# A two-layer SSD and pooling step on one core: another order of the load queue, weight preparation spread over scans 0 to 5, and one step more between a prepared half's loads and their sum

## The chip, the cores and the metric

The kernel runs on one core of a Trainium2 chip. The metric is the device time of one execution in microseconds (us). The kernel before took 1622.03 us, the median of three runs (1621.26 to 1628.29). The engines are called as in the profile: PE (matrix multiplies; PEld its weight loads), DVE and ACT (vector and scalar work on tiles), POOL, and SP, which here only issues DMAs.

## The reference

One inference step of two mixer layers with a prompt of 1024 tokens and 8 sample sequences of 8 tokens. Layer 0 is a Mamba-2 layer (SSD), layer 1 a causal pooling layer; each is adaLN, RMSNorm, projection, mixer, gate, out projection, residual. Cut to what matters here:

```python
mod = silu(c) @ ada_w[i] + ada_b[i]              # shift, scale, gate of layer i
hn  = rmsnorm(x, norm_g[i]) * (1 + scale) + shift
# layer 0
z, xbc, dt = split(hn @ w_in)                    # z 2048, x|B|C 4096, dt 32
xs, B, C = split(silu(causal_conv4(xbc)))        # 8 groups of 4 heads, state 128
acum = cumsum(dt * A)                            # in chunks of 128 tokens
y = (C B^T * exp(acum_t - acum_s)) (xs dt) + C exp(acum) h_prev     # scan over chunks
x = x + gate * (groupnorm((y + d*xs) * silu(z)) * norm_g) @ w_out
# layer 1: pooled windows 2, 4, 8, 16 of u, a product per group, * silu(z), @ pool_w_out
```

It also returns the new states (ssm, conv and pool, for prompt and sample).

## The kernel before, in words

All of it is fp32 work done on PE by splitting an operand into a high and a low float32r part; a product is three matmuls (hi x hi, lo x hi, hi x lo). The helper on L103 records every matmul, L106 every transpose, so in the profile PE's rows have these lines and are told apart by their tiles: st (fast pairs of the projections), mm (in-projections of a group during the scans), tr, S and y (the scan), am (adaLN), op (out products), pl (pool). The two out projections are computed by seven block products instead of eight, so for some of them blocks of the weight have to be added or subtracted first.

The program runs in stages. A front part of 108 us sets up the norms; the fast pairs last to about 349 us; eight scans, one for each group of heads, last from there to about 860 us; the out product of layer 0 overlaps the last scans and lasts to about 1000 us; the pool layer and its out product take the rest. Each scan g has four steps p of 256 tokens (L1630 on). While scan g runs, PE is kept at work with units of the next group's in-projection (`units`, L1607, numbers of units in the table PACE; in scans 6 and 7 the units are of the out product) and with blocks of adaLN (`ada`).

- **Weight stream.** A list of weight blocks is loaded in order: `stream_raw` (L130) issues a 512 KB load on SP into one of three buffers wr, L137 for projection weights (wr<-win), L141 for adaLN weights (wr<-adaG). `stream_split` makes of it wh (ACT, L160) and wl (DVE, L161). `stream_next` splits the next block and loads those behind it. `ada_block` (L260) takes two raw blocks for sixteen am matmuls, ACT copies the result to mp (L273), two small matmuls follow, and DVE makes shf and scl of it (L292, L293).
- **Weight preparation.** `prep_step` (L1176) is called at each scan step with (g, p), and once ahead of the scans with None. It works on halves of summed weight blocks, 16 in all (NPREP is 8 weights). For one half: two loads of 256 KB (SP, L1195, wp<-wout), the sum of the two (DVE, L1186), the high part (ACT, L1181), the low part (DVE, L1182), and a store of 512 KB to DRAM (SP, L1183, wpd<-wp). The out product reads them back with `ow_load` (L1205). The table PREP (L42) says how many halves are begun at a step; the sum of a half belongs to the call after the one that loads it, the split and store to the call after that.
- **Decay broadcast.** `scan_ac` (L539) loads the running sums of a step, broadcast to all partitions (SP, L542, acb<-acd, 512 KB), into the one buffer acb. ACT reads it for ea (L575), M (L580) and, last, cd (L583). The next acb load can go only then.
- **Convolution and its stores.** `proj_evict` moves mm out of PSUM (ACT, L456, L458); the conv is ACT L364 and DVE L366 to L369; POOL gathers the new conv state into ncv (L371) and SP stores it (L407). `silu_burst` (L412) does the silu of the next group's tiles between two scans, and the transposes tr of the next scan read them. Some tiles were made earlier and are reloaded (L430, xbc<-xbd, the table MOVED).
- **Scan.** POOL L602 and DVE L603 carry the state h; L606 stores the last one (hpT). L1132 loads gated rows (b<-gyd) for the out product, ACT L1140 splits them.

What sets the order: PE's instructions in the scans are pinned in program order. On ACT, DVE, POOL and SP a scheduler places the instructions by program order and by its own estimate of when their operands are ready. Each engine then works through its list in order and waits at each row for what the row needs. SP's list is in order as well, and a DMA there may also wait for one of a ring of eight completion semaphores, that is for the landing of the eighth DMA before it.

Of the kernel before, what the change touches and what calls it, by code (L numbers as in the profile page):

```python
# [40 lines left out]
NPREP = 8  # L41
PREP = {None: 4, (0, 0): 2, (0, 1): 2, (0, 2): 1, (0, 3): 1, (1, 3): 1, (2, 3): 2, (3, 3): 2, (4, 3): 1}  # L42
OWTAGS = (("wr", "wr"), ("wh", "wl"), ("wh", "wl"))
# [68 lines left out]
class Build:  # L112
# [147 lines left out]
    def ada_block(self, src, raws=None):  # L260

        nc = self.nc
# [7 lines left out]
        if own:  # L270
            self.slots.free(*own)
        mp = self.cp.tile([P, 256], F32, tag="mp", bufs=1, name=self.name("mp"))
        nc.scalar.activation(mp, pm[:, :256], AF.Copy)  # L273
# [103 lines left out]
    def proj_open(self, g):  # L377
# [3 lines left out]
        return dict(g=g, scv=scv, ncv=ncv, ti=(16 + g, 24 + g, 2 * g, 2 * g + 1), out=[])  # L381

    def proj_begin(self, G, ii):
        nc = self.nc
        raw = self.raw_tile()
        nc.gpsimd.memset(raw[:, 0:3], 0.0)
        nc.gpsimd.tensor_copy(raw[:, 1027:1115].rearrange("p (b w) -> p b w", w=11)[:, :, 0:3], G["scv"][:, ii])
        return raw

    def proj_end(self, G, ii, raw, ahead=False):  # L390
        dst = self.slots.get("xbc")
        self.conv_tile(G["ti"][ii], raw, dst, G["ncv"][:, ii])
        g, nt = G["g"], self.io["ncT"][G["g"]]
# [8 lines left out]
        if ii == 3 and not ahead:  # L402
            kept = [i for i in range(4) if (g, i) not in MOVED]
            for a in kept:
                if a - 1 not in kept:
                    n = next(i for i in range(a, 5) if i not in kept)
                    self.nc.sync.dma_start(nt[:, a:n], G["ncv"][:, a:n])  # L407

# [15 lines left out]
    def proj_group(self, G):  # L424

        nc = self.nc
        for ii in range(4):
            if (G["g"], ii) in MOVED:
                dst = self.slots.get("xbc")
                nc.sync.dma_start(dst, self.xbd[G["g"], ii])  # L430
                G["out"].append(dst)
                continue
            w = self.stream_next()
            raw = self.proj_begin(G, ii)
# [153 lines left out]
    def scan_state(self, s, p):  # L588

        nc, gp = self.nc, self.gs  # L590
# [4 lines left out]
        for cc in range(2):  # L595
            h, Sv = s.h[-1], S[:, 256 * cc:256 * cc + 256].rearrange("p (r q) -> p r q", r=4)
            hn = gp.tile([P, 4, 64], F32, tag="h", bufs=3, name=self.name("h"))
# [6 lines left out]
            s.h.append(hn)  # L604
        if p == 3:
            nc.sync.dma_start(self.io["hpT"][s.g], hn.rearrange("p r q -> p (r q)"))  # L606

# [568 lines left out]
    def prep_step(self, key):  # L1176

        nc = self.nc
        summed, loaded = self.preps
        for i, h, op, t, v in summed:  # L1180
# [6 lines left out]
        new = []  # L1187
        for _ in range(min(PREP.get(key, 0), 2 * NPREP - self.prepn)):
# [7 lines left out]
            new.append((i, h, op, t, v))  # L1196
        self.preps = loaded, new

# [134 lines left out]
    def run(self):  # L1333
# [22 lines left out]
        with tc.tile_pool(name="cp", bufs=1) as self.cp, tc.tile_pool(name="wp", bufs=1) as self.wp, \  # L1356
# [11 lines left out]
            self.wpd = [dr.tile([P, 2, 8, P], F32, tag=f"wpd{i}", name=f"wpd{i}") for i in range(NPREP)]  # L1368
            self.preps, self.prepn = ([], []), 0
            self.x1d = [dr.tile([P, TOK], F32, tag=f"x1d{i}", name=f"x1d{i}") for i in range(8)]  # L1370
# [186 lines left out]
    def fills(self):  # L1557
# [9 lines left out]
        for j, _ in enumerate(pr):  # L1567
# [4 lines left out]
            if j < 8:  # L1572
                yield
        self.ow_load()
        self.x = [None] * 8
        yield from self.out_fill()
# [40 lines left out]
    def scan(self, s, fill):  # L1617

        g = s.g
        last, after = self.scans[g - 1] if g else None, self.scans[g + 1] if g < 7 else None  # L1620
        for p in range(4):
# [10 lines left out]
            if p < 3:  # L1632
                self.scan_decay(s, p + 1)
                if p < 2:
                    self.scan_ac(s, p + 2)
                elif after:
                    self.scan_ac(after, 0)
            self.units(fill, b)
            if p == 3 and after:
                self.silu_burst(after)  # L1640
            self.scan_y(s, p, self.sample_y if p == 3 else None)
            if p == 2:
                self.sample_front(s)
                self.sample_inter(s)
# [7 lines left out]
            elif p == 3:  # L1652
                if g < 7:
                    self.sample_decay(s)
                else:
                    self.gate_rows(s)
            self.units(fill, min(c, 1))
            for _ in ada:
                pass
# [345 lines left out]
```

## Time and profile before

| | before |
|---|---|
| median of three runs | 1622.03 us (1621.26 to 1628.29) |
| profiled execution | 1621.86 us |
| its span (what the trace shows) | 1620.0 us |
| PE busy | 1568.6 us, 97% |
| DVE, ACT, POOL busy | 1307.7 (81%), 803.4 (50%), 491.8 (30%) us |
| DMA moved | 295.80 MB, mean 183 GB/s |

The span is the time in the trace from the first to the last instruction; the 1.86 us between it and the execution's own time lie around it. A wait is written as "engine, line, what it waited for: total us, times, longest". A row of a timeline is the start in us, the length, the engine, the line, the operation, what it writes and reads, the shape, the count, and in brackets the idle time before it with its releaser. For a row that groups several instructions the length is that of the group. PEclk in a table of windows is the TensorE clock that was granted, 1.00 at full speed.

### The profile page before, as it was taken

To read this page: it belongs to the slowest core of one execution; us is meant where nothing else is said; L and a number is where in the kernel's file an instruction comes from. 1 tells how busy PE (TensorE), PEld (TensorE's weight loads), DVE (VectorE), ACT (ScalarE), POOL (GpSimd) and SP (SyncE) were. 2 spreads that over 40 slices of the span, in tenths; PEclk is the share of its full clock that TensorE was granted. 3 is DMA by queue.
4 is the path that set the end of the run, shared out by engine and by line. 5 is a ranking of instruction groups with operands and counts; after the bars stand their busy time and mean duration, and the time that the engine had idled before them with its cause. 6 is when DMAs were issued, how large, how long until landed. Compare 5 with 4: busy or idle time off the path is not lost.

```text
span 1620.0 us, 31607 instructions
## 1 busy us (share of the span) xinstructions
PE 1568.6 (97%) x12495; PEld 1508.3 (93%) x12495; DVE 1307.7 (81%) x2095; ACT 803.4 (50%) x1426; POOL 491.8 (30%) x508
## 2 busy tenths in 40 slices
PE   8999999997999999999998999999999999999997
PEld 6899999996988888988887999999999999999997
DVE  6876787857888889888896999888889867667876
ACT  6663343446667667666653367523232334233355
POOL 0134555511121221111110003765666640000231
PEclk9999999998999999999998999999999999999999
DMA  8422222378675675677889763233323379466673
GB/s 350 164 100 94 87 84 85 111 245 289 225 251 186 207 255 187 215 262 246 320 282 306 194 161 118 71 115 113 115 102 105 108 236 380 135 179 178 162 164 115
DMA packets 118651, 295.80 MB, mean 183 GB/s; under 512 B 22860, under 2 KB 46824, under 8 KB 118504
## 3 DMA queue, kind: packets, MB, share of 16 engines
q1 hardware_dynamic: 110440, 270.32, 48.8%
q0 software_dynamic: 5760, 19.01, 6.7%
q10 hardware_dynamic: 2304, 4.46, 0.7%
q8 instruction: 98, 1.61, 0.4%
q14 instruction: 49, 0.40, 0.1%
HBM read 222.93 MB, written 68.59 MB: 180 GB/s over the span
## 4 chain that ended last, share of the span: by engine, by line
PE 77%; DVE 7%; DMA 7%; ACT 5%; issue 2%; POOL 1%; SPq 0%; DVEq 0%; ACTq 0%; POOLq 0%
PE st L103 32%; PE mm L103 18%; PE op L103 15%; PE y L103 3%; DMA wp<-wout 2%; PE pl L103 2%; DMA acb<-acd 2%; PE S L103 2%; PE am L103 1%; ACT M L580 1%; DMA wr<-pout 1%; PE tr L103 1%; PE ms L103 1%; DVE raw L366 1%; PE tr L106 1%
## 5 line engine op out<-in xcount | busy, mean ns | idle before, releaser
L103 PE MATMUL op<-b,w 128*128 128x272 f32 x2688 | 350.0, 292 | 15.6 <-ACT w L1231 7.1
L103 PEld LDWEIGHTS op<-b,w 128*128 128x128 f32 x2688 | 343.4, 191 | 21.3 <-ACT w L1231 7.7
L103 PE MATMUL st<-hh,w 128*128 128x272 f32 x1664 | 323.2, 289 | 0.0
L103 PEld LDWEIGHTS st<-hh,w 128*128 128x128 f32 x1664 | 265.4, 189 | 0.3 <-issue 0.3
L103 PE MATMUL st<-t,w 128*128 128x272 f32 x1872 | 242.7, 288 | 1.3 <-POOL w L197 1.3
L103 PE MATMUL st<-hl,w 128*128 128x272 f32 x832 | 240.6, 289 | 0.0
L103 PEld LDWEIGHTS st<-t,w 128*128 128x128 f32 x1872 | 237.4, 188 | 1.5 <-POOL w L197 1.5
L103 PE MATMUL mm<-hh,wh 128*128 128x364 f32 (+1 forms) x528 | 183.7, 348 | 2.1 <-ACT wh L160 2.1
L103 PE MATMUL mm<-hh,wl 128*128 128x364 f32 (+1 forms) x528 | 175.1, 332 | 0.3 <-DVE wl L161 0.3
L103 PE MATMUL mm<-hl,wh 128*128 128x364 f32 (+1 forms) x528 | 174.9, 331 | 0.0
L103 PEld LDWEIGHTS st<-hl,w 128*128 128x128 f32 x832 | 156.8, 188 | 0.0
L195 ACT ACTIVATE w<-wr 128x512 fp32r<-128x512 f32 x104 | 65.6, 631 | 179.6 <-PE st L103 143.7
L602 POOL TENSOR_TENSOR hd<-h,cd 128x256 f32<-128x256 f32 x56 | 58.5, 1044 | 225.8 <-DVE h L603 142.5
L103 PEld LDWEIGHTS mm<-hh,wh 128*128 128x128 f32 x528 | 100.7, 191 | 14.0 <-issue 9.5
L366 DVE SCALAR_TENSOR_TENSOR raw<-raw,vec,raw 128x1112 f32<-128x1112 f32 x64 | 91.2, 1426 | 17.5 <-ACT raw L364 17.0
L197 POOL TENSOR_TENSOR w<-wr,w 128x512 fp32r<-128x512 f32 x52 | 91.4, 1757 | 44.2 <-ACT w L195 44.2
L103 PEld LDWEIGHTS mm<-hl,wh 128*128 128x128 f32 x528 | 100.7, 191 | 0.7
L103 PEld LDWEIGHTS mm<-hh,wl 128*128 128x128 f32 x528 | 100.4, 190 | 0.8 <-DVE wl L161 0.8
L1256 DVE SCALAR_TENSOR_TENSOR x<-op,gat,x 128x272 f32<-128x272 f32 (+1 forms) x160 | 73.1, 480 | 26.9 <-PE op L103 23.0
L580 ACT ACTIVATE M<-acb,tka 128x128 f32<-128x128 f32 x256 | 81.1, 389 | 24.6 <-PE y L103 13.1
L974 DVE TENSOR_TENSOR u<-st,u 128x272 f32<-128x272 f32 x174 | 67.6, 411 | 31.6 <-PE st L103 29.8
L197 DVE TENSOR_TENSOR w<-sw,w 128x512 fp32r<-128x512 f32 x78 | 79.2, 1016 | 14.6 <-ACT w L195 14.4
(279 smaller groups left out, 3210.5 us busy)
## 6 DMA issues: line engine op xcount, KB each, us to landing
wr<-win SPq DMA_DIRECT2D x48, 512.0 KB, 4.1
acb<-acd SPq DMA_DIRECT2D x32, 512.0 KB, 4.6
wr<-pin SPq DMA_DIRECT2D x32, 512.0 KB, 3.5
wr<-pout SPq DMA_DIRECT2D x28, 512.0 KB, 4.5
wr<-wout SPq DMA_DIRECT2D x20, 512.0 KB, 5.7
wr<-pout POOLq DMA_DIRECT2D x20, 512.0 KB, 5.9
x<-xT SPq DMA_DIRECT2D x16, 544.0 KB, 6.7
zsd<-z SPq DMA_DIRECT2D x16, 544.0 KB, 2.7
```

The lines of the kernel that those rows point to most:

```text
L103: return self.pin(self.build.nc.tensor.matmul(*a, **k))
L106: return self.pin(self.build.nc.tensor.transpose(*a, **k))
L195: self.nc.scalar.activation(hi, src, AF.Copy)
L197: eng.tensor_tensor(out=lo, in0=src, in1=hi.bitcast(F32), op=ALU.subtract)
L366: nc.vector.scalar_tensor_tensor(out=acc[:, :n], in0=raw[:, k:k + n], scalar=w[k], in1=acc[:, :n], op0=ALU.mult, op1=ALU.add)
L580: nc.scalar.activation(M[:, r, t], acb[:, r, t], AF.Relu, bias=self.tka[cc][:, col + r:col + r + 1], scale=-1.0)
L602: nc.gpsimd.tensor_tensor(out=hd, in0=h, in1=cd[:, :, cc].unsqueeze(2).to_broadcast([P, 4, 64]), op=ALU.mult)
L974: nc.vector.tensor_tensor(out=out, in0=x, in1=y, op=ALU.add)
L1256: ins = nc.vector.scalar_tensor_tensor(out=x[e][:, a:a + pn], in0=ps[:, :pn], scalar=g, in1=x[e][:, a:a + pn], op0=ALU.mult, op1=ALU.add)
```

## The change

The changed kernel differs in these points:

- **PREP** spreads the 16 halves: 2 ahead of the scans (4 before), one at each step of scan 0 (2, 2, 1, 1 before), one at the steps 1 and 3 of the scans 1 to 5 (before one or two at step 3 of the scans 1 to 4).
- `prep_step` keeps three lists and not two: loaded at one call, passed on at the next, summed at the one after, split and stored at the one after that.
- `ada_block` issues, right after its am matmuls, the loads of up to three next blocks of the stream.
- The store of the conv state is put into a list `late` and issued at the next `proj_begin`; the reload of MOVED tiles waits until tile 3 of the group; the store hpT moves from `scan_state` to a later point of the step.
- `scan_ac` for the step after next moves from behind `scan_decay` to behind the units and `scan_y`.

```diff
-PREP = {None: 4, (0, 0): 2, (0, 1): 2, (0, 2): 1, (0, 3): 1, (1, 3): 1, (2, 3): 2, (3, 3): 2, (4, 3): 1}
+PREP = {None: 2, **{(g, p): 1 for g in range(6) for p in range(4) if g < 1 or p in (1, 3)}}
...
         if own:
             self.slots.free(*own)
+        else:
+            for i in range(self.wpos, min(self.wpos + 3, len(self.items))):
+                if len(self.wraw) < 3:
+                    self.stream_raw(i)
...
     def proj_begin(self, G, ii):
         nc = self.nc
+        for dst, src in self.late:
+            nc.sync.dma_start(dst, src)
+        self.late = []
...
-                    self.nc.sync.dma_start(nt[:, a:n], G["ncv"][:, a:n])
+                    self.late.append((nt[:, a:n], G["ncv"][:, a:n]))
...
             if (G["g"], ii) in MOVED:
-                dst = self.slots.get("xbc")
-                nc.sync.dma_start(dst, self.xbd[G["g"], ii])
-                G["out"].append(dst)
+                G["out"].append(None)
                 continue
+            if ii == 3:
+                for i in range(3):
+                    if G["out"][i] is None:
+                        G["out"][i] = self.slots.get("xbc")
+                        nc.sync.dma_start(G["out"][i], self.xbd[G["g"], i])
...
-        summed, loaded = self.preps
+        summed, loaded, asked = self.preps
...
-        self.preps = loaded, new
+        self.preps = loaded, asked, new
...
             if p < 3:
                 self.scan_decay(s, p + 1)
-                if p < 2:
-                    self.scan_ac(s, p + 2)
-                elif after:
-                    self.scan_ac(after, 0)
             self.units(fill, b)
             if p == 3 and after:
                 self.silu_burst(after)
             self.scan_y(s, p, self.sample_y if p == 3 else None)
+            if p < 2:
+                self.scan_ac(s, p + 2)
+            elif p == 2 and after:
+                self.scan_ac(after, 0)
```

PE's list is the same in both kernels. The others move, and three places show how. In the order rows an engine's instructions stand as they are issued, with the line, the operation, the tile written, the tiles read and the shape; the changed kernel's lines are up to 16 higher for the same statement (acb is L542 before and L554 after, the halves' loads L1195 and L1205, their stores L1183 and L1193, while the stream's L137 and L141 stay).

SP in scan 0, before, up to the second adaG load with the win load behind it:

```order
L542 DMA acb_4214<-acd 128x4x256
L636 DMA h_95_4423<-h0T 128x1024
L636 DMA h_96_4425<-h0T 128x1024
L639 DMA acs_4427<-acd 128x4x64
L1183 DMA wpd_161<-wp_4129 256x1x512
L1183 DMA wpd_161<-wp_4132 256x1x512
L542 DMA acb_4330<-acd 128x4x256
L1183 DMA wpd_162<-wp_4135 256x1x512
L1183 DMA wpd_162<-wp_4138 256x1x512
L1195 DMA wp_4445<-wout 128x512 x2
L1195 DMA wp_4448<-wout 128x512 x2
L542 DMA acb_4495<-acd 128x4x256
```

Behind these stand the second adaG load and the win load. The first of the acb rows here is the second of the scan. And after, the same stretch, up to the same two loads:

```order
L141 DMA wr_4319<-adaG 128x1024
L646 DMA h_91_4412<-h0T 128x1024
L554 DMA acb_4208<-acd 128x4x256
L646 DMA h_92_4414<-h0T 128x1024
L649 DMA acs_4416<-acd 128x4x64
L1205 DMA wp_4422<-wout 128x512 x2
L444 DMA xbc_4541<-xbd_145 128x1088
L1193 DMA wpd_161<-wp_4129 256x1x512
L554 DMA acb_4365<-acd 128x4x256
L141 DMA wr_4376<-adaG 128x1024
L137 DMA wr_4378<-win 128x1024
```

The adaG load and the win load stand behind the scan's third acb load and not behind the fourth, with one half's loads and one store between the second and the third acb, and none between the third and the pair.

ACT at the boundary between the scans 1 and 2, where the silu of the second group's tiles (L412 before, L421 after), a half (wp), the next weights (wh), the evictions (raw<-mm) and the convolution (raw<-raw,vec) meet. Before:

```order
L675 ACTIVATE Bs_6154<-tr_6143,kc 128x128 x2
L273 ACTIVATE mp_6186<-am_6177 128x256
L412 ACTIVATE xbc_5971<-xbc_5971 128x1088
L1181 ACTIVATE wp_6238<-wp_6238 128x512
L160 ACTIVATE wh_6261<-wr_6259 128x1024
L456 ACTIVATE raw_6023<-mm_6192 128x296
L458 ACTIVATE raw_6023<-mm_6192 128x8x8
L364 ACTIVATE raw_6220<-raw_6023,vec 128x1112
L1181 ACTIVATE wp_6241<-wp_6241 128x512
L456 ACTIVATE raw_6267<-mm_6270 128x364
```

Two halves pass here, the first ahead of the weights, the evictions and the convolution. After:

```order
L685 ACTIVATE Bs_6136<-tr_6125,kc 128x128 x2
L277 ACTIVATE mp_6172<-am_6159 128x256
L421 ACTIVATE xbc_5950<-xbc_5950 128x1088
L160 ACTIVATE wh_6240<-wr_6168 128x1024
L468 ACTIVATE raw_6002<-mm_6178 128x296
L470 ACTIVATE raw_6002<-mm_6178 128x8x8
L368 ACTIVATE raw_6206<-raw_6002,vec 128x1112
L1191 ACTIVATE wp_6223<-wp_6223 128x512
L468 ACTIVATE raw_6246<-mm_6249 128x364
```

One half passes, and it stands behind the convolution's ACT part.

DVE at the same boundary, after (shf and scl are adaLN's; the sum is L1196, its low part L1192, the convolution L370 to L373):

```order
L296 TENSOR_SCALAR shf_274<-am_6159,vec 128x9
L297 TENSOR_SCALAR scl_276<-am_6159,adab_271,vec 128x9
L161 TENSOR_TENSOR wl_6241<-wr_6168,wh_6240 128x1024
L615 TENSOR_TENSOR h_6229<-hd_6230,S_6226 128x256
L1196 TENSOR_TENSOR wp_6223<-wp_6223 128x512
L370 SCALAR_TENSOR_TENSOR raw_6206<-raw_6002,vec,raw_6206 128x1112
L615 TENSOR_TENSOR h_6233<-hd_6234,S_6226 128x256
L370 SCALAR_TENSOR_TENSOR raw_6206<-raw_6002,vec,raw_6206 128x1112
L1192 TENSOR_TENSOR wp_6223<-wp_6223 128x512
```

Before, the sum and low part of a first half stood ahead of shf, and the sum of a second between scl and the first h; now one sum stands between the first h and the convolution's first row, and the weights' wl ahead of it.

In the scans 6 and 7 the acb load of one step stands behind four b loads where it stood behind two. From the end of scan 7 on the lists of all engines are the same in both kernels.

More of the change, by code (lines that the diff above doesn't have):

```diff
@@ L381, in proj_open @@
         return dict(g=g, scv=scv, ncv=ncv, ti=(16 + g, 24 + g, 2 * g, 2 * g + 1), out=[])
+    late = ()
     def proj_begin(self, G, ii):
         nc = self.nc
+        for dst, src in self.late:
+            nc.sync.dma_start(dst, src)
+        self.late = []
         raw = self.raw_tile()
@@ L604, in scan_state @@
             s.h.append(hn)
-        if p == 3:
-            nc.sync.dma_start(self.io["hpT"][s.g], hn.rearrange("p r q -> p (r q)"))
     def scan_evac(self, s, q, src, tok):
@@ L1368, in run @@
             self.wpd = [dr.tile([P, 2, 8, P], F32, tag=f"wpd{i}", name=f"wpd{i}") for i in range(NPREP)]
-            self.preps, self.prepn = ([], []), 0
+            self.preps, self.prepn = ([], [], []), 0
             self.x1d = [dr.tile([P, TOK], F32, tag=f"x1d{i}", name=f"x1d{i}") for i in range(8)]
@@ L1574, in fills @@
         self.ow_load()
+        for dst, src in self.late:
+            self.nc.sync.dma_start(dst, src)
+        self.late = []
         self.x = [None] * 8
@@ L1657, in scan @@
             self.units(fill, min(c, 1))
+            if p == 3:
+                self.nc.sync.dma_start(self.io["hpT"][g], s.h[-1].rearrange("p r q -> p (r q)"))
             for _ in ada:
```

## The prediction

> **What bounds the kernel now.** I read the busy table first, then PE's waits by stretch, then the timelines of the places where PE waits. The busy table and PE's waits over the whole span (columns: engine, line, what it waited for, total us, times, longest us) come first.
>
> ```profile
> PE 1568.6 (97%) x12495; PEld 1508.3 (93%) x12495; DVE 1307.7 (81%) x2095; ACT 803.4 (50%) x1426; POOL 491.8 (30%) x508
> ...
> PE am L103 <- DMA wr<-adaG: 7.7, 1, 7.7
> ...
> PE op L103 <- ACT raw L456: 3.6, 1, 3.6
> PE mm L103 <- ACT wh L160: 2.1, 1, 2.1
> ...
> PE mm L103 <- DVE wl L161: 0.3, 1, 0.3
> ```
>
> PE is the bound at 97%. Its own list of instructions does not change with this edit, so all that the edit can give is idle time, or time at a lowered TensorE clock behind idle time. The largest single wait is one load, wr<-adaG, in scan 0. Here are PE's waits in the scans 0 to 5 (402 to 740 us), which hold the boundaries between two groups.
>
> ```profile
> PE tr L106 <- ACT xbc L412: 4.7, 3, 2.4
> PE am L103 <- ACT mp L273: 1.0, 1, 1.0
> PE y L103 <- DVE h L603: 0.9, 1, 0.9
> ```
>
> Together 6.6 us. So the two places in play are scan 0 and the boundaries. This is PE in scan 0 (start, us, engine, line, operation, tiles, count, idle time before and its releaser).
>
> ```profile
> 383.29 0.64 PE L103 MATMUL am<-wr,scp 128*32 128x256 f32 x8
> 391.65 1.08 PE L103 MATMUL am<-wr,scp 128*32 128x256 f32 x8 [7.72 <-DMA wr<-adaG]
> 394.81 0.67 PE L103 MATMUL mm<-hh,wh 128*128 128x364 f32 x1 [2.08 <-ACT wh L160]
> ...
> 396.07 0.67 PE L103 MATMUL mm<-hh,wl 128*128 128x364 f32 x1 [0.28 <-DVE wl L161]
> ...
> 398.66 0.51 PE L103 MATMUL mm<-hl,wh 128*128 128x364 f32 x1
> 398.96 0.50 PE L103 MATMUL mm<-hh,wl 128*128 128x364 f32 x1
> ...
> 399.63 0.33 PE L103 MATMUL mm<-hh,wl 128*128 128x364 f32 x1
> 399.80 0.33 PE L103 MATMUL mm<-hh,wh 128*128 128x364 f32 x1
> ```
>
> PE wanted the second adaG load at 383.9 (383.29 + 0.64) and had it at 391.65; the input weights behind it came late too. After the wait the same eight am matmuls take 1.08 us where they took 0.64, and matmuls start 0.30 us apart (398.66 to 398.96) where later they start 0.17 apart (399.63 to 399.80). SP's issues tell why the load is late.
>
> ```profile
> 365.76 0.38 SPq L542 DMA_DIRECT2D acb<-acd  x1
> ...
> 375.86 0.39 SPq L542 DMA_DIRECT2D acb<-acd  x1
> 376.35 1.98 SPq L1183 DMA_DIRECT2D wpd<-wp  x2
> 378.43 3.54 SPq L1195 DMA_DIRECT2D wp<-wout  x4
> 385.75 0.38 SPq L542 DMA_DIRECT2D acb<-acd  x1
> 386.18 0.50 SPq L141 DMA_DIRECT2D wr<-adaG  x1
> 386.77 0.38 SPq L137 DMA_DIRECT2D wr<-win  x1
> ```
>
> The adaG load leaves at 386.18, right behind the fourth acb broadcast, and the win load 0.6 us after it. SP issues in order, and each acb load waits for ACT to have read the one before (there is one acb buffer). The load isn't waiting for its own buffer: it stands behind a broadcast that only the scan's next step lets go.
>
> **The change, scan 0.** In the order of the changed kernel the pair adaG and win stands directly behind the third acb, not the fourth, and four halves' loads (two ahead of the third acb, two behind it) have left the stretch before it. The three acb issues above lie about 10 us apart (365.76, 375.86, 385.75), so one acb earlier alone puts the pair near 376.5. Ahead of the first ea the order now has ACT copy no half at all, where it stood still for a sum (ACT's timeline):
>
> ```profile
> 358.33 0.63 ACT L1181 ACTIVATE wp<-wp 128x512 fp32r<-128x512 f32 x1 [3.63 <-DVE wp L1186]
> ```
>
> These 3.63 us go, so the third acb leaves about 372 and not 375.86, and the pair about 373 to 376.5. Landing took 5.4 us for this adaG load (386.18 to 391.6) and about 3 us more passed until PE had the split win weights at 394.81. So adaG is there at 378 to 382 against 383.9 when PE asks for it, and the split weights at 382 to 385 against 384.4 (0.44 of am work later). I take the whole stall as gone: 7.72 + 2.08 + 0.28 = **10.1 us**. With it goes the lowered clock: the am matmuls' 1.08 - 0.64 = 0.44, and from 394.81 to 399.3 less the 0.28 some 4.2 us of matmuls starting at 0.30 and not 0.17, that is 4.2 x (1 - 0.17/0.30) = 1.8. Sum 2.3, and **12.4 us** for scan 0. What is late next is that win weight: if the pair leaves at 376.5, up to 1 us remains. These two windows (us, busy us of PE, PEld, DVE, ACT, POOL with counts, granted clock, DMA share, GB/s) show the DMA in the stretch, and the clock there:
>
> ```profile
> 339.00:402.00 63.00, 52.80 (x387) 49.03 (x386) 41.30 (x65) 35.23 (x75) 6.27 (x12) 0.92 0.91 306
> 389.00:400.00 11.00, 5.99 (x25) 4.63 (x26) 7.51 (x9) 6.70 (x15) 0.00 (x0) 0.53 0.90 296
> ```
>
> At 0.91 busy a load that goes out earlier could crawl. [...] But here bytes leave the stretch: four halves of 0.5 MB, some 2 MB of the 306 GB/s, 6.5 us of transfer time.
>
> **The change, boundaries.** The boundary between scans 1 and 2, on ACT, DVE and PE:
>
> ```profile
> 541.03 0.63 ACT L1181 ACTIVATE wp<-wp 128x512 fp32r<-128x512 f32 x1 [4.27 <-DVE wp L1186]
> ...
> 552.07 1.11 ACT L412 ACTIVATE xbc<-xbc 128x1088 f32<-128x1088 f32 x1 [4.68 <-DVE xbc L369]
> ```
>
> ```profile
> 540.31 0.69 DVE L1186 TENSOR_TENSOR wp<-wp 128x512 f32<-128x512 f32 x1 [2.35 <-DMA wp<-wout]
> ```
>
> ```profile
> 550.59 0.27 PE L106 MATMUL tr<-kc,xbc 128*128 128x128 f32 x1
> 553.23 1.12 PE L106 MATMUL tr<-kc,xbc 128*128 128x128 f32 x4 [2.37 <-ACT xbc L412]
> ```
>
> The chain is load, sum, ACT's copy, and behind it in ACT's order the eviction and the convolution (L364, then L366 to L369 on DVE), whose silu at 552.07 PE's transposes wait for. In the changed order one half is handled here and not two, and ACT's copy of it stands behind L364. That takes 4.27 us of ACT's wait and DVE's 2.35 out of the way of the convolution, more than the 2.37 that PE waited. So I let the gaps of this kind go: 4.7 + 1.0 + 0.9 = 6.6, and the lowered clock behind the longest, which shows in this window:
>
> ```profile
> 552.90:556.40 3.50, 3.17 (x14) 3.17 (x15) 3.50 (x5) 3.47 (x8) 0.00 (x0) 0.51 0.41 157
> ```
>
> 3.5 x (1 - 0.17/0.30) = 1.5 us. The granted clock is half behind a gap of 2.37 us. [...]
>
> Each of six boundaries now carries one half. The nearest row is the 1.0 us (am behind ACT's mp) of the boundary 0 to 1, which had one half before: so each may still cost from 0 to 0.95. DVE's sum still stands ahead of L366 in its order, ACT's copy no longer stands ahead of L364; I take a third, 6 x 0.95 / 3 = **1.9 us**. Boundaries: 6.6 + 1.5 - 1.9 = **6.2 us**.
>
> **What else moves.** The half handled in the middle of a scan (step 1 of each of the scans 1 to 5) costs DVE 0.69 + 0.69 and ACT 0.63 in stretches where PE has mm matmuls in hand, four us at a time; I cost it at nothing, and a DVE wait on its load up to 3.1 us long would be felt by the y matmuls as the 0.95 above. The deferred ncT stores, the hpT store and the xbc reload issue 0.3 to 0.5 us each on SP and nobody on PE's path waits for them there; nothing. In scans 6 and 7 one acb load now stands behind two more b loads. SP, ACT and PE there before:
>
> ```profile
> 745.24 0.80 SPq L1132 DMA_DIRECT2D b<-gyd  x2
> ...
> 763.82 0.37 SPq L542 DMA_DIRECT2D acb<-acd  x1
> ```
>
> ```profile
> 763.59 0.20 ACT L583 ACTIVATE cd<-acb 128x8 f32<-128x8 f32 x1
> ...
> 769.64 0.40 ACT L580 ACTIVATE M<-acb,tka 128x128 f32<-128x128 f32 x1 [3.50 <-DMA acb<-acd]
> ```
>
> This acb is on the path to the 3.6 us wait of op behind ACT raw. Two more issues are 0.80 us: **0.8 us** lost, bounded by 0 and, if the buffers of those b tiles come free later, by half the 3.5 again, 1.8; the other way the 3.6 could go with 1.5 of clock. The out product, the pool layer and its product are ordered as before: nothing.
>
> Sum: -12.4 - 6.2 + 0.8 = -17.8 us from the profiled execution's 1621.86 (span 1620.0 and 1.86 around it), which is 0.2 under the median of 1622.03. **1604.1 us**.
>
> **The rivals.**
>
> *Only scan 0 is cured.* The added step between load and sum is to let the load land, but the scheduler puts the sum close behind its load again, and DVE goes on meeting it:
>
> ```profile
> DVE wp L1186 <- DMA wp<-wout: 18.5, 10, 3.1
> ```
>
> Ten such waits in the scans; in the changed order the sum is again the next wp row on DVE, ahead of the convolution. Then the one-half boundaries, six of them, give back what the two-half ones took: 1621.86 - 12.4 + 0.8 = 1610.3. It is also the case in which the change does not do what it says. Against it: only one half per boundary, and ACT's copy is out of the way.
>
> *Scan 0 stays.* The pair goes out earlier and lands no earlier, since DMA is 0.91 busy there, or it waits for its buffer instead: then the boundaries alone remain, 1621.86 - 6.2 + 0.8 = 1616.5. Against it: the 2 MB that leave.
>
> *Slower: acb becomes the late load.* Its issue now stands in program order behind a unit of the next group's matmuls and the scan's y, where before it stood ahead of both. These are ACT's waits for it, and the sizes of a unit and a y (the chain's rows):
>
> ```profile
> ACT ea L575 <- DMA acb<-acd: 32.8, 16, 5.1
> ...
> 417.83 4.00 PE mm L103 x24
> 421.83 2.36 PE y L103 x48
> ```
>
> ACT waits for acb 16 times already, so it has no slack there, and it holds PE's evictions in order behind it. Should the load go out 4.00 + 2.36 us later each time, a unit in hand covers 4.00 and 2.36 reach PE: 16 x 2.36 = 37.8, and 1621.86 - 17.8 + 37.8 = 1641.9. It decides from the point where acb's issue lies more than 4 us behind ACT's cd. Against it: acb left 0.2 us behind cd (763.59 + 0.20 to 763.82), being tied to the one buffer and not to its place in the program, and in the changed order it stands directly behind few other issues.
>
> **How the numbers follow.** Measurements of this kernel tell about 0.5%, 8.1 us, from no change: under 1613.9 is faster, over 1630.1 slower. The forecast has 0.50, only scan 0 0.28, scan 0 stays 0.15, slower 0.06, and 0.01 for the rest. Low end: 1621.86 - 12.4 - 8.1 - 5.1 (the 3.6 and its 1.5 of clock) = 1596. High end: the first rival with all bounds against it (1.0 at scan 0, 1.0 more at 774, about 1.5 of new mid-scan waits) 1614. This leaves out most of the second rival and all of the third, 2 in 10. Faster: 0.50 + 0.27 = 0.77; same 0.17; slower 0.06.
>
> **What would show it.** Right: no wait of am for adaG in scan 0, adaG issued before 378, granted clock 1.0 between 389 and 400; no wait of tr for xbc over 1 us, and clock 1.0 behind each boundary. Wrong: a PE wait on wh or wr in scan 0 (the win weight was the later one), tr still waiting 1 to 2 us with DVE waiting for wp ahead of L366 (first rival), or ACT's waits for acb longer than 5.1 and op or mm waiting for ACT raw more than once (third rival).

## The result, and the profile after

The changed kernel took 1611.23 us (median of four runs, 1611.03 to 1612.29) where the kernel before took 1621.64 us beside it: a ratio of 0.9928, 95% interval 0.9902 to 0.9954. That is 10.4 us, and the range of the prediction holds it; 17.8 us were forecast. Measured again on another chip the ratio was 0.9931 (0.9917 to 0.9946). One run of the experiments (of the kernel with tied sums and mp on DVE at step 3, 1891.69 us at a mean granted clock of 0.75 where the others of its kernel had 0.99) is left out of its figures as a slow one. The profiled execution of the changed kernel took 1611.03 us, its span 1609.3 us, so 10.7 us of span are to be accounted for.

PE's longest waits after, in three stretches (339 to 402, 402 to 740, and 740 to 900 us):

```profile
PE am L103 <- ACT mp L277: 2.1, 1, 2.1
```

```profile
PE am L103 <- ACT mp L277: 3.5, 2, 2.0
PE tr L106 <- ACT xbc L421: 2.0, 3, 1.2
```

```profile
PE op L103 <- ACT w L1241: 3.7, 1, 3.7
PE op L103 <- ACT raw L468: 2.9, 1, 2.9
```

The wait of 7.7 us for adaG is gone, and so are those for wh and wl. The tr waits fell from 4.7 to 2.0. New is a kind of wait that before had 1.0 us in the scans 0 to 5: am behind mp, 2.1 + 3.5 us now. The load queue in scan 0 shows why the first is gone (SP's timeline):

```profile
371.89 0.39 SPq L554 DMA_DIRECT2D acb<-acd  x1
372.33 0.50 SPq L141 DMA_DIRECT2D wr<-adaG  x1
372.93 0.38 SPq L137 DMA_DIRECT2D wr<-win  x1
```

The pair leaves at 372.33 where it left at 386.18, and the third acb at 371.89 where the prediction put it at about 372. PE's busy time and clock in the stretch of scan 0 that the prediction shows for before:

```profile
339.00:402.00 63.00, 60.95 (x506) 57.02 (x506) 43.91 (x70) 38.30 (x82) 10.12 (x16) 1.00 0.90 303
```

PE is busy 60.95 of 63 us (52.80 before) at full clock. Since PE's list is the same in both kernels, the same instruction can be looked up in both traces, and the difference of its starts is the lead that the change has gained so far. Four such instructions before and after, beside the matmul at 398.66 that the prediction quotes:

```profile
478.13 0.33 PE L103 MATMUL mm<-hl,wh 128*128 128x364 f32 x1
...
675.89 0.76 PE L106 MATMUL tr<-kc,xbc 128*128 128x128 f32 x5 [0.87 <-ACT xbc L412]
...
739.92 0.33 PE L103 MATMUL mm<-hl,wh 128*128 128x360 f32 x1
...
774.30 0.90 PE L103 MATMUL op<-b,w 128*128 128x272 f32 x4 [3.58 <-ACT raw L456]
```

```profile
386.08 0.33 PE L103 MATMUL mm<-hl,wh 128*128 128x364 f32 x1
...
471.83 0.35 PE L103 MATMUL mm<-hl,wh 128*128 128x364 f32 x1
...
662.80 0.77 PE L106 MATMUL tr<-kc,xbc 128*128 128x128 f32 x5 [0.40 <-ACT xbc L421]
...
731.29 0.33 PE L103 MATMUL mm<-hl,wh 128*128 128x360 f32 x1
...
764.82 1.51 PE L103 MATMUL op<-b,w 128*128 128x272 f32 x7 [2.91 <-ACT raw L468]
```

The lead is 12.6 us behind the stall of scan 0 (398.66 - 386.08), 6.3 in scan 1 (478.13 - 471.83), 13.1 at the boundary from scan 4 to 5 (675.89 - 662.80), 8.6 behind the boundary from 5 to 6 (739.92 - 731.29), 9.5 at the first long wait of op (774.30 - 764.82), and 10.7 at the end. So scan 0 gave what was forecast, and two stretches took 10.8 us back: 6.3 between 386 and 472 us, 4.5 between 663 and 731 us. These are the waits of am in them:

```profile
390.63 0.61 PE L103 MATMUL am<-kc,mp 128*128 128x9 f32 x4 [2.05 <-ACT mp L277]
...
467.67 0.61 PE L103 MATMUL am<-kc,mp 128*128 128x9 f32 x4 [1.48 <-ACT mp L277]
...
726.00 0.61 PE L103 MATMUL am<-kc,mp 128*128 128x9 f32 x4 [2.02 <-ACT mp L277]
```

The windows behind them show what the clock adds (columns as before; the granted clock is the third number from the end):

```profile
390.00:394.00 4.00, 3.37 (x24) 3.27 (x25) 4.00 (x8) 3.97 (x12) 0.00 (x0) 1.00 1.00 393
468.00:472.00 4.00, 4.00 (x15) 3.71 (x15) 1.76 (x5) 2.96 (x6) 0.74 (x5) 0.57 0.95 361
726.00:731.50 5.50, 5.50 (x29) 5.50 (x30) 4.99 (x9) 5.50 (x13) 0.00 (x0) 0.69 0.87 319
```

Behind the first the clock stayed full, behind the other two it fell, though one of them is a gap of 1.48 us. What ACT did ahead of mp at the three places, in order:

```profile
387.71 0.63 ACT L1191 ACTIVATE wp<-wp 128x512 fp32r<-128x512 f32 x1 [1.07 <-DVE wp L1196]
389.25 1.06 ACT L587 ACTIVATE ea<-acb 128x1024 f32<-128x1024 f32 x1 [0.91 <-DMA acb<-acd]
390.21 0.36 ACT L277 ACTIVATE mp<-am 128x256 f32<-128x256 f32 x1
```

```profile
462.91 0.63 ACT L1191 ACTIVATE wp<-wp 128x512 fp32r<-128x512 f32 x1 [2.32 <-DVE wp L1196]
...
464.94 1.28 ACT L421 ACT_TABLE_LOAD   x1
466.23 1.11 ACT L421 ACTIVATE xbc<-xbc 128x1088 f32<-128x1088 f32 x1
467.25 0.36 ACT L277 ACTIVATE mp<-am 128x256 f32<-128x256 f32 x1
```

```profile
723.14 1.11 ACT L421 ACTIVATE xbc<-xbc 128x1088 f32<-128x1088 f32 x1 [2.80 <-DVE xbc L373]
724.27 1.28 ACT L422 ACT_TABLE_LOAD   x1
725.57 0.38 ACT L277 ACTIVATE mp<-am 128x256 f32<-128x256 f32 x1
```

At 390 mp stands behind an ea that waited for the fourth acb. At 467 it stands behind a table load and a silu, and these behind ACT's copy of the half of the middle of the scan, which waited 2.32 us for DVE's sum. At 726 it stands behind the silu of the next group, which waited for the convolution; and the convolution on DVE waited for a half's load:

```profile
716.99 0.69 DVE L1196 TENSOR_TENSOR wp<-wp 128x512 f32<-128x512 f32 x1 [4.01 <-DMA wp<-wout]
717.59 1.37 DVE L370 SCALAR_TENSOR_TENSOR raw<-raw,vec,raw 128x1112 f32<-128x1112 f32 x1
```

One correction to the names: the boundary at 553 us before, which the sections above call that between the scans 1 and 2, is the one between the scans 2 and 3 (by the table of before, two halves are begun at step 3 of scan 2, and two are handled there); the one that the prediction calls 0 to 1, with 1.0 us of am behind mp, is that between the scans 1 and 2.

### The profile page after: what moved, and what is told of

It is laid out like the page before. It is cut to its first block, busy times and chain, and to the rows that moved or that the text cites. A ratio compares the mean times of both kernels' runs of the same rounds, so it can differ in the third digit from the quotient of the medians.

```text
span 1609.3 us, 31627 instructions
## 1 busy us (share of the span) xinstructions
PE 1568.3 (97%) x12495; PEld 1505.9 (94%) x12495; DVE 1303.6 (81%) x2095; ACT 802.6 (50%) x1426; POOL 488.1 (30%) x508
## 4 chain that ended last, share of the span: by engine, by line
PE 65%; DMA 14%; DVE 8%; ACT 7%; issue 3%; SPq 1%; POOL 1%; DVEq 0%; ACTq 0%; POOLq 0%
PE st L103 32%; PE op L103 14%; PE mm L103 11%; DMA acb<-acd 4%; DMA wp<-wout 4%; PE pl L103 2%; ACT M L592 2%; DMA x<-xT 1%; PE y L103 1%; DMA wr<-pout 1%; DVE raw L370 1%; DMA row<-gyd 1%; DMA wpd<-wp 1%; PE am L103 1%; PE S L103 1%
## 5 line engine op out<-in xcount | busy, mean ns | idle before, releaser
L103 PEld LDWEIGHTS op<-b,w 128*128 128x128 f32 x2688 | 342.1, 190 | 20.9 <-ACT w L1241 4.3
L614 POOL TENSOR_TENSOR hd<-h,cd 128x256 f32<-128x256 f32 x56 | 54.0, 964 | 227.6 <-DVE h L615 151.6
L370 DVE SCALAR_TENSOR_TENSOR raw<-raw,vec,raw 128x1112 f32<-128x1112 f32 x64 | 90.3, 1410 | 17.1 <-ACT raw L368 16.7
```

Source lines behind the costliest of these rows:

```text
L103: return self.pin(self.build.nc.tensor.matmul(*a, **k))
L370: nc.vector.scalar_tensor_tensor(out=acc[:, :n], in0=raw[:, k:k + n], scalar=w[k], in1=acc[:, :n], op0=ALU.mult, op1=ALU.add)
L614: nc.gpsimd.tensor_tensor(out=hd, in0=h, in1=cd[:, :, cc].unsqueeze(2).to_broadcast([P, 4, 64]), op=ALU.mult)
```

## The experiments

The theory after the result: scan 0 is cured by the place of the pair adaG, win in SP's queue; at the boundaries PE loses time where a half's sum stands on DVE ahead of the convolution and waits there for its load; and the rest is mp, last in ACT's queue. The rivals: that bytes had to leave the DMA; that the number of halves at a boundary matters and not the place of the sum; that the added step between load and sum is what helps. Ratios are to the kernel before on the same chip, and 0.001 is 1.6 us.

### One half of the change at a time

The table alone, on the kernel before:

```diff
-PREP = {None: 4, (0, 0): 2, (0, 1): 2, (0, 2): 1, (0, 3): 1, (1, 3): 1, (2, 3): 2, (3, 3): 2, (4, 3): 1}
+PREP = {None: 2, **{(g, p): 1 for g in range(6) for p in range(4) if g < 1 or p in (1, 3)}}
```

> The kernel before with the new PREP table alone (two lists, no early adaLN loads, acb and the stores at their old places). In its order the pair adaG, win stands behind the third acb of scan 0, as in the changed kernel. Theory (the table's halves leaving SP's queue move the pair forward, and that is what cures scan 0): no wait of am for adaG, 10 to 12.5 us gained in scan 0, total 1608 to 1613. Rival (the early issue in ada_block is what brings the pair forward): the 7.7 us wait stays, total 1618 to 1622.

Measured: 0.9932 (0.9915 to 0.9949), 1612.34 us. No wait for adaG is left in scan 0; a wait of 2.06 us for wl, the win weight that the prediction named, is. The theory's figure came out, but the next run shows that this is not the only cure.

The early issue in `ada_block` alone, on the kernel before:

```diff
         if own:
             self.slots.free(*own)
+        else:
+            for i in range(self.wpos, min(self.wpos + 3, len(self.items))):
+                if len(self.wraw) < 3:
+                    self.stream_raw(i)
```

> The kernel before with the early issue in ada_block alone. All six halves stay in front, but the second adaG load and its win load stand behind the second acb, one acb earlier still. Theory (the place in SP's queue decides): the wait of am for adaG goes though no byte leaves the stretch, and what is left is the wait for ACT's mp of some 2 us; total 1609 to 1613. Rival (DMA at 0.91 busy decides, the bytes have to leave): the pair goes out earlier and lands late, at least half of the 10 us stays; total 1615 to 1621.

Measured: 0.9933 (0.992 to 0.9945), 1612.20 us. Its SP timeline and its window of scan 0:

```profile
371.03 0.33 SPq L141 DMA_DIRECT2D wr<-adaG  x1
371.46 0.37 SPq L137 DMA_DIRECT2D wr<-win  x1
376.52 0.38 SPq L546 DMA_DIRECT2D acb<-acd  x1
```

```profile
339.00:402.00 63.00, 63.00 (x520) 59.23 (x520) 46.71 (x74) 38.54 (x85) 8.82 (x16) 1.00 0.93 318
```

PE is busy all of the 63 us, and the DMA is as full as it was (0.93 and 318 GB/s; 0.91 and 306 before), with all the halves still there. So the bytes did not have to leave: the place in the queue alone cures scan 0. Either half of the change gains 11 us by itself. In scan 0 both together gain hardly more: the matmul at 398.66 before starts at 388.01 with the table alone, at 386.72 with the early issue alone, at 386.08 with both. The deferred stores and the reload were not tried by themselves.

The changed kernel without the early issue:

> The changed kernel without the early issue in ada_block. Theory (the table alone puts the pair behind the third acb; the early issue is a second cure of the same stall and adds nothing to it): no wait of am for adaG, total within 2 us of the changed kernel. Rival (the early issue carries part of the cure): a wait of 1 us or more for wh or wl in scan 0, 2 to 4 us slower.

Measured: 0.9974 (0.9963 to 0.9985), 1619.42 us. Half of the expectation failed: there is no wait for adaG, wh or wl in scan 0, as the theory says, but the total is 7 us worse than the changed kernel's by the ratio (0.9974 against 0.9931 on the same chip), which neither side foresaw. By the look-up of above it is 5.7 us behind the changed kernel after the boundary from 5 to 6 (737.03 against 731.29) and 9.5 at the op (774.32 against 764.82). Its waits in the scans 1 to 5 say part of where:

```profile
PE tr L106 <- ACT xbc L417: 5.2, 3, 1.7
PE am L103 <- ACT mp L273: 4.2, 2, 2.8
```

On DVE a half's sum stands here at the boundary from scan 2 to 3 ahead of adaLN's shf and scl, as the first of two does in the kernel before, and further from the convolution's end than in the changed kernel; the sums wait for their loads 26.9 us in all (20.9 in the changed kernel). So in the changed kernel the early issue also moved the sum. It is not alone in placing it: with the table alone, without the early issue, the sum stands behind scl, as in the changed kernel.

### The place of the sum

The sum tied behind the last convolution on DVE, first for all halves of the changed kernel, as the edit shows, then from scan 2 on (the same tie with the condition `key and key[0] > 1`):

```diff
-            nc.vector.tensor_tensor(out=v[:, 0].bitcast(F32), in0=v[:, 0].bitcast(F32), in1=v[:, 1].bitcast(F32), op=op)
+            with self.tc.issue_after(self.last_conv.ins):
+                nc.vector.tensor_tensor(out=v[:, 0].bitcast(F32), in0=v[:, 0].bitcast(F32), in1=v[:, 1].bitcast(F32), op=op)
```

> The changed kernel with each half's sum tied behind the last convolution on DVE, so that the scheduler cannot put it close behind its load again. Theory (the first rival of the prediction holds at single boundaries: DVE meets the load ahead of the convolution): the PE waits at 543 (1.22) and 726 (2.02, with 2 us of lowered clock) go, 4 to 6 us gained, total 1605 to 1607; the wait at 467 (1.48, with 1.7 of clock) goes too if the half in the middle of the scan causes it, then 1602 to 1604. Rival (the silu and ACT's own order make these waits, not the half): 1610 to 1612.

Measured: 0.995 (0.9936 to 0.9965), 1614.45 us. The expected gain did not come, and the interval overlaps the changed kernel's. The waits named are gone (467, 543) or small (0.63 at 726), but others came elsewhere. In scan 0 acb is now issued behind a further adaG load, and mp behind it waits 3.01 us; S waits 2.00 us for DVE in scan 1; and near 808 us op waits 3.21 us for a b tile.

> The changed kernel with the sum tied behind the last convolution from scan 2 on only; the scans 0 and 1 keep the changed kernel's order. Theory (hoisted sums make the boundary waits; what the run with all sums tied lost, it lost in scans 0 and 1 and in the b loads of scan 7): the waits at 543 and 726 go or fall under 0.7, those at 390 and 467 stay; PE is 12 to 13 us ahead of the kernel before at 764 us where the changed kernel is 9.5; total 3 to 4 us under the changed kernel unless the b wait near 808 comes (5 us), then 1 to 2 us over it. Rival (the late sums push loads and stores into each other everywhere): no lead at 764 us.

Measured: 0.9932 (0.9918 to 0.9947), 1612.01 us, no different from the changed kernel. The tr waits fell to 0.2 us, but the wait of am at 726 only to 1.41 and not under 0.7. PE was 3.0 us ahead of the changed kernel at the same op (761.81 against 764.82), near the 2.5 to 3.5 us expected, and lost it again near 808 us:

```profile
PE op L103 <- ACT b L1150: 3.7, 2, 3.2
PE op L103 <- DVE b L1151: 2.3, 2, 1.4
```

It is not the load that is late: in this trace the last b<-gyd load ahead of the wait left SP at 794.58 us and landed at 803.96. ACT's copy (L1150) waits for DVE's sum of the b tile:

```profile
807.81 0.72 DVE L1148 TENSOR_TENSOR raw<-b 128x544 f32<-128x544 f32 x1
```

DVE was at work ahead of it, with three rows of x (L1267) and a wait for POOL among others; the tie changed DVE's order here too. Why the scheduler chose this order was not tried and stays open.

The same tie on the kernel before with the early issue (the old table, two lists):

> The kernel before with the early issue in ada_block and with the sums tied behind the last convolution from scan 2 on; the old table, two lists, acb at its old place. Theory (scan 0 is cured by the place in the queue, the boundaries by the place of the sum, and these two add up): the tr waits at 544 (1.48 and 1.5 of clock), 607 (1.85) and 669 (0.99) and the y waits of 0.5 go; 5 to 7 us under the run with the early issue alone, a ratio of 0.988 to 0.991 to the kernel before. Rival (two halves at a boundary are the cause, wherever the sum stands): as the early issue alone, 0.993.

Measured: 0.9882 (0.9863 to 0.99), 1603.36 us, as the theory said (the profiled execution was the slowest of five, 1608.41 us). Its boundary from scan 2 to 3 on DVE:

```profile
531.46 1.59 DVE L370 SCALAR_TENSOR_TENSOR raw<-raw,vec,raw 128x1112 f32<-128x1112 f32 x1 [0.28 <-ACT raw L368]
...
533.31 1.37 DVE L370 SCALAR_TENSOR_TENSOR raw<-raw,vec,raw 128x1112 f32<-128x1112 f32 x1
534.71 1.28 DVE L371 SCALAR_TENSOR_TENSOR xbc<-raw,vec,raw 128x1024 f32<-128x1024 f32 x1
535.91 0.28 DVE L373 SCALAR_TENSOR_TENSOR xbc<-raw,vec,raw 128x64 f32<-128x64 f32 x1
```

No sum stands among the rows and no DMA is waited for, though the old table begins two halves here: the two sums run at 554.91 us, behind the convolution that follows this one. The rival that counts halves falls. The tie took ACT's copies out of the boundary together with the sums, so this run does not tell the two apart.

### The added step

The changed kernel with two lists again:

```diff
-        summed, loaded, asked = self.preps
+        summed, loaded = self.preps
...
-        self.preps = loaded, asked, new
+        self.preps = loaded, new
```

> The changed kernel with the step between load and sum taken back (two lists). Theory (the scheduler puts the sum behind its load anyway, so the step does nothing or little): the same waits at the boundaries, total within 2 us of the changed kernel. Rival (the step gives the load time to land): DVE's waits for wp rise from 23 us to over 30, boundary waits of 2 us and more, 5 us slower.

Measured: 0.9892 (0.9875 to 0.9909), 1606.33 us. Neither expectation: without the step the kernel is some 6 us faster than with it (0.9931 and 0.9928; the repeat's interval, 0.9917 to 0.9946, does not touch this one's, the first one's, 0.9902 to 0.9954, does by 0.0007). On its own chip the nearest yardstick is the changed kernel with acb's load at its old place, told of below: 0.9942 (0.9925 to 0.9958), which does not touch it. The boundary from scan 2 to 3 on DVE, changed kernel and then this one:

```profile
533.43 0.41 DVE L615 TENSOR_TENSOR h<-hd,S 128x256 f32<-128x256 f32 x1
536.61 0.69 DVE L1196 TENSOR_TENSOR wp<-wp 128x512 f32<-128x512 f32 x1 [2.77 <-DMA wp<-wout]
```

```profile
533.80 1.37 DVE L370 SCALAR_TENSOR_TENSOR raw<-raw,vec,raw 128x1112 f32<-128x1112 f32 x1
535.67 0.69 DVE L1196 TENSOR_TENSOR wp<-wp 128x512 f32<-128x512 f32 x1 [0.50 <-DMA wp<-wout]
```

With three lists the sum stands ahead of both long rows of the convolution and waits 2.77 us; with two it stands behind both and waits 0.50. At this boundary the step in the program did not keep the sum from its load; the scheduler brought it back, and to a worse place. DVE's waits ahead of the sums from 402 to 740 us are 22.7 us with the step and 17.0 without; the profile puts 20.9 and 10.3 of them down to the loads and names no releaser for the rest. In scan 1 the step did delay a sum, from 450.52 to 462.18 us, and with it ACT's copy from 453.18 to 462.91, ahead of the silu and mp: this is the wait at 467, and it is where the two kernels part first. By the look-up the kernel with two lists is 3.5 us ahead of the changed one there (468.32 against 471.83), 3.9 at the boundary from 4 to 5 (658.90 against 662.80), 6.6 behind that from 5 to 6 (724.73 against 731.29) and 4.9 at the end. PE's waits from 402 to 740 us, beside the place of the sum at the boundary from 2 to 3:

| kernel | the sum on DVE, seen from the convolution | tr waits for the silu, us | am waits for mp, us |
|---|---|---|---|
| changed, no early issue | ahead of shf and scl | 5.2 | 4.2 |
| before | one ahead of shf, a second ahead of conv | 4.7 | 1.0 |
| before, early issue alone | one ahead of shf, a second just ahead of conv | 4.3 | 3.2 |
| before, table alone | just ahead of conv | 4.5 | 2.7 |
| changed (and its repeat) | just ahead of conv | 2.0 (2.3) | 3.5 (2.9) |
| changed, acb at its old place | just ahead of conv | 2.4 | 4.5 |
| changed, mp on DVE | just ahead of conv | none | 3.4 |
| changed, two lists | behind both long rows | none | 3.0 |
| changed, sums tied from scan 2 on | behind all of it | 0.2 | 2.7 |
| changed, all sums tied | behind all of it | none | 0.6 |
| changed, two lists, mp on DVE at step 3 | behind both long rows | 0.6 | 2.7 |
| before, early issue, sums tied | behind all of it | none | 5.1 |
| before, early issue, sums tied, mp on DVE at step 3 | behind all of it | none | 4.0 |

Some of these kernels are told of below. Wherever the sum stands behind the long rows, tr waits 0.6 us at most, and that at another boundary (from 0 to 1). With the sum ahead of them the tr waits run from none to 5.2 us, with the same place just ahead of the convolution too (none with mp off ACT): ACT's order has a part in them as well, and the place of the sum alone does not set their size.

### acb's place, and mp

acb's load back at its old place in the program of the changed kernel:

> The changed kernel with acb's load back at its old place in the program. Theory (the one buffer and not the place in the program ties it): SP's order in scan 0 is the same, the waits at 390 and 467 stay, total within 1.5 us of the changed kernel. Rival (acb's later place makes ea late and mp behind it): the wait at 390 goes, 2 us gained there, and 4 us and more over all the scans.

Measured: 0.9942 (0.9925 to 0.9958), 1613.72 us; the wait at 390 is 1.78 us, the one at 467 is 1.39. The ratio lies 0.0011 over the repeat of the changed kernel, 1.8 us where 1.5 were allowed, and the intervals overlap widely. The theory holds: the place in the program moved nothing on SP in scan 0, and no cost of it is seen.

The copy mp on DVE, everywhere in the changed kernel:

```diff
-        nc.scalar.activation(mp, pm[:, :256], AF.Copy)
+        nc.vector.tensor_copy(mp, pm[:, :256])
```

> The changed kernel with the adaLN copy mp on DVE and not on ACT. Theory (the new PE waits are ACT's order: mp stands behind an ea that waits for acb, or behind the silu): the waits at 390 (2.05) and 467 (1.48 and 1.7 of clock) go, the one at 726 turns into a wait of tr for the silu or shrinks; total 1604 to 1607. Rival (the copy is late because am or its PSUM buffer is late, or DVE is as late as ACT): same waits, 1610 to 1613.

Measured: 0.9956 (0.994 to 0.9972), 1615.39 us. The wait at 467 is gone, the one at 390 doubled to 4.14 us: on DVE the copy comes later still. So ACT's order made the wait at 467, but DVE is no better place in scan 0. As an edit it is a miss.

The copy on DVE at step 3 of a scan alone, on the kernel before with early issue and tied sums, and on the changed kernel with two lists:

> The kernel before with the early issue, the sums tied behind the last convolution from scan 2 on, and the adaLN copy mp on DVE at step 3 of a scan alone (scans 1 and 5, where it stood behind the silu and the table load on ACT). Theory (ACT's order at the boundary makes the last waits of am for mp): the waits at 479 (2.23) and 721 (1.53) shrink to under 1 us and the lowered clock behind the first (1.5 us) goes; 3 to 4 us under the run without it, a ratio of 0.985 to 0.987. Rival (DVE's copy is as late, behind the gating of the y rows, or tr waits for the silu anyway): 0.988 to 0.989.

> The changed kernel with two lists and the adaLN copy mp on DVE at step 3 alone. Theory: the waits at 480 (1.23) and 721 (1.73 and 1.3 of clock) shrink, that at 390 (2.42, mp behind an ea that waits for acb, at step 2) stays; 1.5 to 3 us under the run with two lists alone, 0.987 to 0.988. Rival: 0.989 or more.

Measured: 0.9871 (0.9854 to 0.9888), 1602.71 us, and 0.9907 (0.9895 to 0.992), 1607.94 us. The first is not told apart from 0.9882 without the copy, the second not from 0.9892. In the first the wait at 479 fell from 2.23 to 1.24 and that at 721 went, but the next wait of am grew from 1.29 (at 739) to 1.85 (at 735) and a tr wait of 1.23 us came at 741. In the second the waits at 480 and 721 are 1.14 and 1.52, where they were 1.23 and 1.73. The theory is not borne out beyond the single waits.

The changed kernel once more, as a yardstick for these:

> The changed kernel once more, on the same chip as the three beside it. Theory: 0.993 of the kernel before, so the kernel with two lists (0.989 elsewhere) is faster than the changed kernel by more than the noise. Rival (the gain of two lists was the chip's): 0.990 or less.

Measured: 0.9931 (0.9917 to 0.9946), as the theory said. Its profile is a warning: in this execution, the slowest of six, the same kernel showed the am waits in other sizes (2.53 us near 392, none at 467, 2.62 near 728, 3.48 near 748) and a span of 1613.8 us. A single wait under 3 us in one profile is not settled by that profile; the waits told of above as gone or made are those that the order explains too.

## Why the prediction was right or wrong

**Scan 0: right, to 0.2 us, and for the reason given.** 12.4 us were forecast, 12.6 came (11.6 in the repeat's profile, 398.66 - 387.02, so the 0.2 is luck in part). The third acb was put at about 372 and left at 371.89. One step of it was not needed: the 2 MB that leave. The early issue alone gained as much with the bytes still there. An order cured the stall on a full DMA (0.93 busy), because the late load waited for its issue and not for bandwidth. Hardly any bandwidth came of it (318 GB/s in the window of that run, 306 in that of the kernel before), and none was needed.

**What is late next in scan 0: missed.** The prediction named the win weight. It was mp, behind an ea that waits for the fourth acb: 2.05 us. In the kernel before this stood hidden in the stall. The win weight was the later one only with the table alone (2.06 us). In the run with the early issue alone, where mp stands ahead of ea on ACT, there is no such wait.

**Boundaries: the chain was right, the size wrong.** Forecast were 6.2 us. Between scan 1 and the boundary from 4 to 5 the lead rose by 13.1 - 6.3 = 6.8. But the 6.3 before that were lost (2.05 us at 390, 1.48 at 467 with the clock at 0.57 behind it, and smaller ones), and the boundary from 5 to 6, which got a half that it had not had, lost 13.1 - 8.6 = 4.5 where the term for the six boundaries had 1.9 for all. The step that failed is "so each may still cost from 0 to 0.95; I take a third": the row it went by was a half whose sum waited 3.15 us where this one waited 4.01, and the fall of the clock behind the gap was left out of that price. From 386 us to 731 us the change loses 12.6 - 8.6 = 4.0 where 6.2 more were forecast, and this is the whole difference to the forecast and more. Of the signs that the prediction set, those for scan 0 came (adaG out at 372.33, clock 1.00 from 388 to 400 us). Of those for the boundaries a wrong one did: tr waited 1.22 us at 543.40, behind the sum that waited 2.77 us for its load ahead of the convolution.

**The half in the middle of a scan: wrong at scan 1.** It was costed at nothing, with DVE's wait for its load as the only risk. What it cost came by another path: DVE's sum had no wait, but ACT's copy waited for it ahead of the silu and mp. The traces bear this out. Where ACT's copy waits 2.1 to 2.3 us there, am waits 1.3 to 1.5 near 467 (the changed kernel, the ones without the early issue, with acb at its old place, with sums tied from scan 2 on). Where the copy waits 0.45 (the repeat) or stands elsewhere (two lists, all sums tied), am does not wait. In the changed kernel the wait and its clock are 3.3 us of lead: 9.6 before them (464.94 - 455.30), 6.3 behind them.

**Scans 6 and 7: a loss of 0.8 forecast, a gain seen.** From 731 us to the end the lead rises from 8.6 to 10.7. The wait of op behind ACT's w fell from 6.3 to 3.7, but in the repeat it was 6.1. This is within what one profile can tell.

**The first rival was nearly the outcome.** Its time of 1610.3 stands 0.9 from the median, with the mechanism it named at the boundaries: the scheduler puts the sum close behind its load and DVE meets it ahead of the convolution. That the time is so near is luck in part, since the boundaries up to that from 4 to 5 did gain (the 6.8 us of above) and mp at 390 and 467 lost, of which the rival said nothing. The forecast gave it 0.28 and took the better case, since ACT's copy stood behind L364. The sum on DVE still held the boundary from 5 to 6, which the prediction had seen and given a third. The added step cost some 6 us. That neither the forecast nor the rivals said; it was read as harmless.

**The slower rival did not come.** acb's issue stays tied to ACT's cd, and the run with its old place shows no difference. The second rival (scan 0 stays) did not come either.

**The clock.** The prediction took its 1.5 us from one window, 0.51 behind a gap of 2.37 us. In the changed kernel a window had 0.57 behind 1.48 us and another 0.69 behind 2.02, beside 1.00 behind 2.05: the length of a gap did not tell the clock behind it.

## What to carry to other kernels

When a load is late, look first at what stands ahead of it in the queue that issues it: moving the issue one or two broadcasts forward gave 11 us on a DMA that stayed 0.89 to 0.93 busy, and a second cure of the same stall gave hardly anything on top. A stage added in program order is no sure distance in time when a scheduler places the instructions: at the boundaries the sum came back to its load, and in scan 1 it went to where other work had to wait for it; tie the instruction behind the work that it must not delay, and look at its row in the order. And behind a stall that goes, ask what had been hidden in it, with the lowered clock in its price.

## What the runs showed of the hardware

The granted clock does not follow the length of a single gap. In the changed kernel it was 0.57 behind 1.48 us and full behind 2.05 us; in the repeat on another chip, in this window, it was 0.50 behind 2.5 us at the same instruction as the 2.05 (columns as before):

```profile
392.00:397.00 5.00, 4.96 (x19) 4.60 (x20) 4.27 (x8) 4.29 (x12) 0.00 (x0) 0.50 0.94 376
```

Where a gap falls in time may have a part in it, but this was not shown. In the traces of the kernel before and of the changed kernel the granted clock is 1.00 or 0.50, and each low stretch up to 880 us is 3.41 us long or two or three times that (10.24 us from 389.08 in the kernel before, 6.83 us from 854.14 in the changed kernel). In the changed kernel it falls at 468.43, 727.85, 744.91 and 765.39 us, which lie 259.42, 17.06 and 20.48 us apart, that is 76, 5 and 6 times 3.413 us. The changed kernel around the wait of 1.48 us:

```profile
465.02:468.43 3.41, 1.93 (x13) 1.61 (x12) 2.95 (x6) 3.40 (x4) 0.00 (x0) 1.00 1.00 297
468.43:471.85 3.42, 3.42 (x12) 3.15 (x11) 1.57 (x5) 2.38 (x5) 0.59 (x5) 0.50 0.97 369
471.85:475.26 3.41, 3.41 (x27) 3.18 (x28) 2.90 (x4) 1.57 (x3) 1.60 (x1) 1.00 0.89 270
```

The 1.48 us lie whole in the first stretch, which PE filled to 57%, and the next is at half clock. The gap of 2.05 us is cut by 389.93 us, which lies 23 times 3.413 us ahead of the fall at 468.43; PE was busy 60% and 79% of the stretches on its two sides (2.06 of 3.42 and 2.71 of 3.41 us), and the clock stayed at 1.00. But the gap of 2.02 us lies on both sides of 724.43 us, 3.42 us ahead of the fall at 727.85, and there the clock fell. PE's busy share in these stretches does not tell it either: the one from 741.50 us of the changed kernel, 74% busy, was followed by a low one, and the one from 386.51 us, 60% busy, was not.

A price for a short wait of PE has to be given with and without some 1.5 to 2 us of lowered clock, an estimate from these stretches (3.41 us at 0.50 are 1.7).
